# Sliding windows by DMA: staged batches in two half-block units instead of whole blocks, and one clear for all semaphores

## Chip, cores and metric

The kernel runs on 1 core of one Trainium2 chip. The metric is device time in microseconds (us), the median of several runs. Lower is better.

## What is computed

The input `x` holds 32 batches of 4096 rows of 256 float32 numbers. Every batch is cut into 127 windows of 64 rows that start 32 rows apart, so neighbouring windows overlap by half. The output is the list of windows:

```
def reference(x, window_size, stride):            # 64, 32
    batch, length, dim = x.shape                  # 32, 4096, 256
    n_windows = (length - window_size) // stride + 1        # 127
    result = np.zeros((batch, n_windows, window_size, dim), dtype=np.float32)
    for i in range(n_windows):
        start = i * stride
        result[:, i] = x[:, start:start + window_size].copy()
    return result
```

Nothing is calculated. A batch is 128 blocks of 32 rows (32 KB each, 4 MB in all). Window w is block w followed by block w + 1. A batch of output is 127 windows of 64 KB, that is 8.3 MB, and the whole output is 266 MB.

## The kernel before

The kernel consists of DMA transfers alone. It moves the batches in two ways.

**Copied batches.** Twenty of the 32 batches go from DRAM to DRAM. `copy` (L93) starts three DMAs for each of them on the SP queue, for 80, 32 and 15 windows. `COPY_PARTS` also says into how many pieces the 64 KB of a window are cut: 4, 2 and 4, which makes pieces of 16, 32 and 16 KB. Every byte of the output is then read from DRAM once, so most blocks are read twice.

**Staged batches.** Twelve batches (`STAGED`, the odd numbers 1 to 23) go through SBUF on the ACT queue. `load` (L75) brings the 128 blocks of a batch into one tile, one block of 32 KB in each partition. `store` (L83) waits until the tile has been loaded (L88) and writes it to DRAM twice: once into the first halves of the windows, once (half -1) into the second halves. Each DMA of a staged batch is 4 MB, and `start` (L61) cuts its 32 KB rows into pieces of 16 KB. There are five tiles (`BUFS`), used in turn; a load into a tile that was used before first waits (L79) until that tile's earlier stores have ended.

The ACT queue is written out in L139 to L148: load 0, then for each n load n + 1 followed by the two stores of n. One load is always issued ahead of the store that waits.

**The order between the two.** Written as 128 whole blocks, each store of a staged batch reaches a half window too far into the batch before it and the batch after it, and leaves a wrong block there. The neighbours, which are copied batches, put that right by being written later: on the SP queue, a copied batch next to a staged one waits (L137) until the staged batch's stores have ended. `_order` (L102) puts those copies where the wait should be short. Four batches (`EARLY`: 18, 20, 22, 24) are copied first instead, before their neighbours are stored; ACT waits for these once (L146). Their damaged blocks are repaired at the end of the SP queue by seven DMAs of 32 KB (`half`, L46, started in L152 to L158), each after the store that damages the block.

Every DMA adds 16 to a semaphore when it ends, in shares of one for every DMA engine that takes part. `loaded` and `stored` have one semaphore for each tile, and `copied` and `early` one each. At the end SP waits for all stores (L159) and all copies (L161), and clears the twelve semaphores one by one (L162, L163).

Names used below: the SP ring and the ACT ring are what the two queues (q1 and q10 of the profile) hold on each of the 16 DMA engines. A turn of a ring is one packet that it gets from an engine.

Of the kernel before, what the change touches and what calls it, by code (L numbers as in the profile page):

```python
# [1 line left out]

# [4 lines left out]


STAGED = tuple(range(1, 24, 2))
BUFS = 5  # L10

EARLY = (18, 20, 22, 24)

BLOCK_PARTS = 2

COPY_PARTS = ((80, 4), (32, 2), (15, 4))


class _Geometry:


    def __init__(self, x, out, W, S):
        self.B, self.L, self.D = x.shape
        self.x, self.out = x, out
        self.n_win = (self.L - W) // S + 1
        self.n_blk = self.L // S
        self.blk = S * self.D
        self.win = W * self.D
        assert W == 2 * S and self.n_blk == self.n_win + 1 == 128

    def src(self, b, block, dims):

        at = (b * self.n_blk + block) * self.blk
        return bass.AP(self.x.tensor, self.x.offset + at, dims)

    def dst(self, b, half, dims):

        at = b * self.n_win * self.win + half * self.blk
        return bass.AP(self.out.tensor, self.out.offset + at, dims)

    def rows(self, b, w0, n):

        s, d = [[self.blk, n], [1, self.win]], [[self.win, n], [1, self.win]]
        return self.dst(b, 2 * w0, d), self.src(b, w0, s)

    def half(self, b, half, block):  # L46

        dims = [[self.blk // 16, 16], [1, self.blk // 16]]
        return self.dst(b, half, dims), self.src(b, block, dims)


class _Kernel:
    def __init__(self, nc, g, tiles):
        self.nc, self.g, self.tiles = nc, g, tiles
        self.loaded = [nc.alloc_semaphore(f"loaded{i}") for i in range(len(tiles))]
        self.stored = [nc.alloc_semaphore(f"stored{i}") for i in range(len(tiles))]
        self.copied = nc.alloc_semaphore("copied")
        self.early = nc.alloc_semaphore("early")
        self.count = {}

    def start(self, engine, out, in_, sem, parts=1):  # L61
        engine.dma_start(out=out, in_=in_, max_dma_last_dim=65536 // parts).then_inc(sem, 16)
        self.count[id(sem)] = self.count.get(id(sem), 0) + 16

    def all_of(self, engine, sem):
        engine.wait_ge(sem, self.count[id(sem)])

    def slot(self, n):
        return divmod(n, len(self.tiles))

    def after_store(self, engine, n):
        turn, i = self.slot(n)
        engine.wait_ge(self.stored[i], 32 * (turn + 1))

    def load(self, n):  # L75

        g, (_, i) = self.g, self.slot(n)
        if n >= len(self.tiles):
            self.after_store(self.nc.scalar, n - len(self.tiles))  # L79
        src = g.src(STAGED[n], 0, [[g.blk, g.n_blk], [1, g.blk]])  # L80
        self.start(self.nc.scalar, self.tiles[i][:, :], src, self.loaded[i], 2 * BLOCK_PARTS)

    def store(self, n):  # L83

        g, (turn, i) = self.g, self.slot(n)
        self.nc.scalar.wait_ge(self.loaded[i], 16 * (turn + 1))  # L88
        for half in (0, -1):
            dst = g.dst(STAGED[n], half, [[g.win, g.n_blk], [1, g.blk]])  # L90
            self.start(self.nc.scalar, dst, self.tiles[i][:, :], self.stored[i], 2 * BLOCK_PARTS)

    def copy(self, b, sem):  # L93

        w = 0
        for rows, parts in COPY_PARTS:
            self.start(self.nc.sync, *self.g.rows(b, w, rows), sem, parts)
            w += rows
        assert w == self.g.n_win


def _order(B):  # L102


    near = {b for s in STAGED for b in (s - 1, s + 1)}
    order = list(EARLY) + [b for b in range(B) if b not in near and b not in STAGED]
    tied = sorted(near - set(EARLY))
    n = len(order) + len(tied)
    for b in tied:
        behind = max(STAGED.index(s) for s in (b - 1, b + 1) if s in STAGED)  # L110
        order.insert(-(-(2 * behind + 5) * n // (2 * len(STAGED))), b)
    return order


@with_exitstack
def kernel(
    ctx: ExitStack,
    tc: tile.TileContext,
    x: bass.AP,
    window_size: bass.AP,  # L120
    stride: bass.AP,
    out: bass.AP,
):
    nc = tc.nc
    W, S = int(window_size), int(stride)
    g = _Geometry(x, out, W, S)
    assert 0 not in STAGED and g.B - 1 not in STAGED
    pool = ctx.enter_context(tc.tile_pool(name="blocks", bufs=1))
    tiles = [pool.tile([g.n_blk, g.blk], x.dtype, name=f"xb{i}") for i in range(BUFS)]

    with tc.tile_critical():
        k = _Kernel(nc, g, tiles)
        for b in _order(g.B):
            if b not in EARLY:
                for s in (b - 1, b + 1):
                    if s in STAGED:
                        k.after_store(nc.sync, STAGED.index(s))  # L137
            k.copy(b, k.early if b in EARLY else k.copied)
        k.load(0)  # L139
        waited = False  # L140
        last = len(STAGED) - 1
        for n, s in enumerate(STAGED):
            if n < last:
                k.load(n + 1)
            if not waited and (s - 1 in EARLY or s + 1 in EARLY):
                k.all_of(nc.scalar, k.early)  # L146
                waited = True
            k.store(n)  # L148


        k.all_of(nc.sync, k.early)
        for n, s in enumerate(STAGED):  # L152
            if s - 1 in EARLY or s + 1 in EARLY:
                k.after_store(nc.sync, n)
            if s - 1 in EARLY:
                k.start(nc.sync, *g.half(s - 1, 2 * g.n_win - 1, g.n_blk - 1), k.copied)
            if s + 1 in EARLY:
                k.start(nc.sync, *g.half(s + 1, 0, 0), k.copied)  # L158
        for n in range(len(STAGED)):  # L159
            k.after_store(nc.sync, n)  # L160
        k.all_of(nc.sync, k.copied)  # L161
        for sem in [*k.loaded, *k.stored, k.copied, k.early]:  # L162
            nc.sync.sem_clear(sem)  # L163


# [1 line left out]
_INS = ['x', 'window_size', 'stride']  # L167
_OUTS = [((32, 127, 64, 256), 'float32')]

_NUMBERS = {'window_size': 64, 'stride': 32}  # L170


# [26 lines left out]
```

## Time and profile before

| | |
|---|---|
| runs before | 768.57, 766.97, 766.28 us; median 766.97 us |
| profiled execution | 768.4 us, of which the span of the instructions is 766.6 us |
| moved by DMA | 317.70 MB, mean 414 GB/s |
| SP queue (q1) | 10044 packets, 166.70 MB |
| ACT queue (q10) | 9792 packets, 151.00 MB |
| DRAM | 217.02 MB read, 267.35 MB written |
| busy time of the compute engines | 0.2 us (four fills on POOL) |

There is no compute engine to look at. The profile is read by its DMA part: the share of time that the 16 DMA engines are busy, the GB/s of chosen stretches, the packets of each queue, and the waits and issues on the two issuing engines, SP and ACT. The chain of work that ended last follows compute instructions and says nothing here.

### The profile page before, as it was taken

How to read it: one execution, taken by the hardware profiler on the slowest of the kernel's cores; microseconds unless marked ns; L12 is line 12 of the kernel's file. 1: busy time of each engine (PE TensorE's matmuls, PEld its weight loads, DVE VectorE, ACT ScalarE, POOL GpSimd, SP SyncE). 2: the span in 40 equal slices, each digit the busy share in tenths (PEclk: the TensorE clock that was granted, in tenths of full speed). 3: DMA queues.
4: the chain of work that ended last, by engine and by line, in shares of the span. 5: the costliest groups of instructions: out<-in, count | busy, mean ns of one | idle time of the engine just before them, and what ended most of it. 6: DMA issues, size and time to landing. Idle time of an engine off the chain costs nothing. (4 is left out here: it accounts for less than half of the span.)

```text
span 766.6 us, 180 instructions
## 1 busy us (share of the span) xinstructions
POOL 0.2 (0%) x4
## 2 busy tenths in 40 slices
POOL 0000000000000000000000000000000000000000
DMA  8999999999999999999999999999999999999996
GB/s 371 425 410 421 405 428 431 408 411 427 423 415 421 431 415 425 432 408 416 427 420 417 431 420 420 423 428 410 414 427 419 422 428 418 417 428 421 420 406 237
DMA packets 19837, 317.70 MB, mean 414 GB/s; under 512 B 1628, under 2 KB 1628, under 8 KB 1740
## 3 DMA queue, kind: packets, MB, share of 16 engines
q1 hardware_dynamic: 10044, 166.70, 51.9%
q10 hardware_dynamic: 9792, 151.00, 47.3%
q14 instruction: 1, 0.01, 0.0%
HBM read 217.02 MB, written 267.35 MB: 632 GB/s over the span
## 5 line engine op out<-in xcount | busy, mean ns | idle before, releaser
L180 POOL MEMSET const-bfloat16-1.0<- 128x1 bf16 x1 | 0.1, 102 | 0.0
L180 POOL MEMSET const-uint8-127<- 128x1 uint8 x1 | 0.1, 102 | 0.0
L180 POOL MEMSET const-float32-0.0<- 128x1 f32 x1 | 0.1, 99 | 0.2 <-issue 0.2
L180 POOL MEMSET const-float32-1.0<- 128x1 f32 x1 | 0.1, 99 | 0.0
## 6 DMA issues: line engine op xcount, KB each, us to landing
out_dram<-in_x_dram SPq DMA_DIRECT2D x20, 5120.0 KB, 114.8
out_dram<-xb ACTq DMA_DIRECT2D x24, 4096.0 KB, 84.6
xb<-in_x_dram ACTq DMA_DIRECT2D x12, 4096.0 KB, 123.2
out_dram<-in_x_dram SPq DMA_DIRECT2D x20, 2048.0 KB, 116.7
out_dram<-in_x_dram SPq DMA_DIRECT2D x20, 960.0 KB, 97.7
out_dram<-in_x_dram SPq DMA_DIRECT2D x7, 32.0 KB, 48.3
```

What stands on the lines that cost most here:

```text
L180: nc = _bacc.Bacc("TRN2", target_bir_lowering=False, num_devices=1)
```

## The change

A staged batch is no longer moved as whole blocks. Every block is cut in two halves of 16 KB (`BLOCK_PARTS` = 2 columns of the tile), and a unit is one half of all 128 blocks of a batch: 2 MB. The twelve staged batches become 24 units. A unit has a load, two stores, a `loaded` and a `stored` semaphore of its own, so there are ten slots in the same five tiles. The two halves of a batch follow each other. Two units are loaded ahead (`AHEAD` = 2) where one batch was before. The pieces of 16 KB stay as they are. Where SP waited for the stores of a batch, it now waits for both units (`after_batch`). The 22 semaphores, which have consecutive numbers, are cleared by one instruction.

```diff
+BLOCK_PARTS = 2
+AHEAD = 2
...
+        self.slots = len(tiles) * BLOCK_PARTS
+        self.size = g.blk // BLOCK_PARTS
+        self.loaded = [nc.alloc_semaphore(f"loaded{i}") for i in range(self.slots)]
+        self.stored = [nc.alloc_semaphore(f"stored{i}") for i in range(self.slots)]
...
-    def load(self, n):
-        g, (_, i) = self.g, self.slot(n)
-        if n >= len(self.tiles):
-            self.after_store(self.nc.scalar, n - len(self.tiles))
-        src = g.src(STAGED[n], 0, [[g.blk, g.n_blk], [1, g.blk]])
-        self.start(self.nc.scalar, self.tiles[i][:, :], src, self.loaded[i], 2 * BLOCK_PARTS)
+    def after_batch(self, engine, n):
+        for c in range(BLOCK_PARTS):
+            self.after_store(engine, n * BLOCK_PARTS + c)
+    def in_tile(self, unit):
+        t, c = divmod(unit % self.slots, BLOCK_PARTS)
+        return self.tiles[t][:, c * self.size : (c + 1) * self.size]
+    def in_dram(self, at, unit, step):
+        c = unit % BLOCK_PARTS
+        return bass.AP(at.tensor, at.offset + c * self.size, [[step, self.g.n_blk], [1, self.size]])
+    def load(self, unit):
+        g, i = self.g, unit % self.slots
+        if unit >= self.slots:
+            self.after_store(self.nc.scalar, unit - self.slots)
+        src = self.in_dram(g.src(STAGED[unit // BLOCK_PARTS], 0, [[1, 1]]), unit, g.blk)
+        self.start(self.nc.scalar, self.in_tile(unit), src, self.loaded[i])
+    def store(self, unit):
+        g, (turn, i) = self.g, divmod(unit, self.slots)
         self.nc.scalar.wait_ge(self.loaded[i], 16 * (turn + 1))
         for half in (0, -1):
-            dst = g.dst(STAGED[n], half, [[g.win, g.n_blk], [1, g.blk]])
-            self.start(self.nc.scalar, dst, self.tiles[i][:, :], self.stored[i], 2 * BLOCK_PARTS)
+            dst = self.in_dram(g.dst(STAGED[unit // BLOCK_PARTS], half, [[1, 1]]), unit, g.win)
+            self.start(self.nc.scalar, dst, self.in_tile(unit), self.stored[i])
...
-        k.load(0)
-        last = len(STAGED) - 1
-        for n, s in enumerate(STAGED):
-            if n < last:
-                k.load(n + 1)
+        for unit in range(AHEAD):
+            k.load(unit)
+        units = len(STAGED) * BLOCK_PARTS
+        for unit in range(units):
+            if unit + AHEAD < units:
+                k.load(unit + AHEAD)
+            s = STAGED[unit // BLOCK_PARTS]
...
-            k.store(n)
+            k.store(unit)
...
-        for sem in [*k.loaded, *k.stored, k.copied, k.early]:
-            nc.sync.sem_clear(sem)
+        used = sorted(sem.num for sem in [*k.loaded, *k.stored, k.copied, k.early])
+        nc.sync.sem_clear(range(used[0], used[-1] + 1))
```

## The prediction

> **What bounds the kernel now.** I read the page's DMA part first, since no compute engine works. It holds the busy share and the rate of 40 slices (19.2 us each), the packets and the two queues.
>
> ```profile
> DMA  8999999999999999999999999999999999999996
> GB/s 371 425 410 421 405 428 431 408 411 427 423 415 421 431 415 425 432 408 416 427 420 417 431 420 420 423 428 410 414 427 419 422 428 418 417 428 421 420 406 237
> q1 hardware_dynamic: 10044, 166.70, 51.9%
> q10 hardware_dynamic: 9792, 151.00, 47.3%
> ```
>
> The 16 DMA engines are busy 51.9 + 47.3 = 99.2% of 766.6 us, so 760 us, and only the first and last slices show slack. No wait on SP or ACT can be worth more than the remaining 6 us. What the change does to the busy time decides: the bytes, which stay, and the time of a packet. In the packet records of the trace the median packet of 16 KB takes 0.611 us in both queues, one of 32 KB 1.213 us. Summed over all packets, the time above these medians is 18.8 us per engine (sum divided by 16). So the rate in the slices varies between 405 and 432 GB/s, and I ask when it falls. Next I read the rate by stretches, in one cycle of ACT: load of staged batch 3 (ends 168), the two stores of batch 2 (190, 210), load of batch 4 (232). These times are the medians of the 16 completions of each DMA.
>
> ```profile
> 149.00:155.00 6.00, 0.00 (x0) 1.00 0.94 347
> 155.00:165.00 10.00, 0.00 (x0) 1.00 1.00 429
> 165.00:168.00 3.00, 0.00 (x0) 1.00 1.01 344
> 171.00:187.00 16.00, 0.00 (x0) 1.00 1.02 434
> 187.00:190.00 3.00, 0.00 (x0) 1.00 1.01 410
> 190.00:207.00 17.00, 0.00 (x0) 1.00 1.00 427
> 207.00:210.00 3.00, 0.00 (x0) 1.00 1.00 382
> 219.00:229.00 10.00, 0.00 (x0) 1.00 1.01 423
> 229.00:232.00 3.00, 0.00 (x0) 1.00 1.00 350
> 750.00:757.00 7.00, 0.00 (x0) 1.00 0.91 348
> 757.00:764.00 7.00, 0.00 (x0) 1.00 0.41 143
> ```
>
> The last two columns are DMA share and GB/s. Inside a load (429, 423) and inside the stores (434, 427) the rate is the same. It falls where ACT's ring turns: before the end of a load (344, 350), before the end of the second store (382), and after the start of a load (347). Where a store follows a store it hardly falls (410). I call this the cost of a turn of direction. The engines are as busy as before (share about 1.0), the packets of both rings take longer.
>
> At the end, SP's ring is alone from 750 on, slow (348), and then engines finish one after another.
>
> **The change, part by part.** ACT's order before: loads 0 and 1, stores 0, load 2, stores 1 and so on: 11 turns from load to store and 10 back. After: three loads, then two stores and one load in turn: 22 and 21. So 11 turns of each kind are added. The depth is the same: when ACT waits for a load to land, its ring holds two stores and a load behind it (12 MB), after the change four stores and two loads of half the size (12 MB). So no engine runs dry, and the wait on a tile (ten slots, 20 MB) is over long before.
>
> 1. Ends before a turn. I summed packet time above the medians, per engine, from 6 us before to about 2 us after the median completion: 0.47 us at a load's end (10 loads), 0.38 at the end of the second store (10), 0.09 at the end of the first store (11), which has no turn. A turn costs 0.38 + 0.29 over that, a pair 0.67; 11 pairs make +7.4 us, on all engines, thus on the path.
> 2. Starts of loads. From 1 to 12 us after the second store's end the same sum is 0.47 us (from 0.13 to 0.92), over some 0.1 at first stores. The new load lasts about 10 us instead of 20. Either each start costs the whole (11 x 0.36 = +4.0) or the loss belongs to the bytes and is only spread (0). I take the middle, +2.0.
> 3. Completions. 36 DMAs more, each with one 4-byte packet of 9 ns on each engine: +0.3 us.
> 4. One clear. The twelve start 59 ns apart, from 764.93 to 765.58, with nothing beside them: -0.65 us.
> 5. Who ends last. Chained end to start, the records show the engines alternate strictly between the rings, one packet each (an ACT packet followed the SP packet in 6,893 of some 7,600 cases), and a completion packet takes a whole turn. Before, ACT has 36 x (16 + 1) = 612 turns per engine, SP 20 x 28 + 60 = 620 and 14 small ones at the end. ACT starts 3.4 us, some 5 packets, ahead; so SP has 13 turns left alone, which is the stretch from 750 on. After, ACT has 72 x (8 + 1) = 648. SP ends first, and ACT has some 24 turns, 13 us, alone, all stores. ACT-alone stores are not in the trace: between 348 GB/s (nothing gained) and 428 (7 us x (1 - 348/428) = -1.3). I take -0.9, nearer the store rows.
> 6. The last two repairs of 32 KB. SP issues them when the last store has landed:
>
> ```profile
> SPq L62 <- DMA out_dram<-xb: 61.2, 2, 40.2
> SPq L66 <- DMA out_dram<-in_x_dram: 7.7, 1, 7.7
> ```
>
> The wait of 40.2 us ends at 755.3. The repairs then lie behind SP's own copies, whose last packet ends at 763.17, and they land at 764.86: 1.7 us later. With SP's ring empty that cover is gone: the second is issued 0.96 us after the wait, a packet starts 1.07 us after an issue (ACT's first: 0.91 to 1.98), and their packets took 0.08 to 1.3 us. That is 2.1 to 3.4 us after the last store, +0.4 to +1.7; I take +1.1.
>
> Cost nothing: the 36 more issues on ACT (0.44 us each, while its ring holds tens of us of work), and the longer chains of waits on SP at the end (one instruction in 65 ns, during the repairs' flight). SP's copies behind a staged batch wait longer, as ACT's data now falls behind by up to 36 turns, some 40 us by the end. Queued behind these waits are all later copies; the DMAs already in SP's ring hide it, as a copy's first DMA lands 114.8 us after its issue. Without that cover SP's engines' turns would go to ACT, and only the tail could lengthen.
>
> Sum: 7.4 + 2.0 + 0.3 - 0.65 - 0.9 + 1.1 = +9.2 us on 768.4, the profiled execution's time, so 777.6. That run lies 1.4 us above the median of the three; on the median's scale, 776.2.
>
> One rule speaks against the change more strongly. The Trainium skill, DMA: Bandwidth & Descriptors, section Anatomy of one DMA, fits a GpSimd-issued DMA by about 2.0 us fixed plus bytes over 436 GB/s. By that, 36 more DMAs would add 72 us if nothing covered them. The stretches across a store's end show a share of 1.00 or more, so no gap.
>
> The same page, section Queues, rings and completion order, says an engine drains a whole packet, typically 9 to 17 descriptors, from one ring before it switches. By that a half load (8 pieces) would pass in one go and point 5's count of turns would be wrong. The records of this trace alternate after every piece of 16 or 32 KB, and the measurement decides.
>
> **The rivals.**
> - Only the ends change (no rate change): the turns' cost belongs to the bytes loaded. Then +0.3 - 0.65 - 0.9 + 1.1 = -0.15: 766.8 on the median's scale. For it: the starts vary from 0.13 to 0.92. Against it: the inside of a load costs nothing, and the first store's end hardly anything.
> - Faster: engines no longer turn together. A load lasts 10 us per engine instead of 20. Where the spread of the 16 completions reaches that, only about a third of the engines load at a time, direction is mixed evenly, and the bursts of both ends go. Half of the present 13.2 us at turns (4.7 + 3.8 + 4.7 over 10 cycles) saved is -6.6: 760.2. It decides once the spread is about 10 us for most engines; load 5 landed between 291.4 and 300.7, but 14 of 16 within 2.8 us. That speaks against it.
> - Much slower by addresses: pieces of 16 KB are now 32 KB apart in the load and 64 KB apart in the stores, where pairs lay together. If all loads ran as the load's worst rows (347 instead of 412 GB/s over the 247 us of loads), +46 us, about 822. Nothing in the trace shows it, as pieces were separate packets already.
>
> **How the numbers follow.** A measurement of this kernel can tell about 0.3%, or 2.3 us, from no change. Chances: turns cost again, 0.68; only the ends, 0.15; mixing, 0.14; addresses, 0.03. The likeliest gives 776.2 us. Its own range: point 1 by 0.4 to 1.3 of its size (turns of short units may burst less, or both kinds longer), point 2 from 0 to 4.0, points 5 and 6 by their bounds, which is 769 to 782. The range for 8 in 10 reaches down over the second rival but not the third, and up a little: 764 to 783. Faster by over 0.3% (under 764.7): 0.14. Within: nearly all of the second rival and a little of the first, 0.16. Slower: 0.70.
>
> **What would show it.** Right: DMA share still over 99%, mean GB/s some 1% lower, slices more even and nearer 410 than 430, low stretches at the end of every half load; ACT's queue ends last; SP's last wait for stores ends a few us before the end and the wait for the copies (7.7 us) shrinks to 2 or 3; one clear. Wrong: slices at 425 and over (turns cost nothing, or less when mixed), idle DMA engines in the middle (the depth does not hold), or SP's ring alone at the end as before (point 5).

## The result and the profile after

The changed kernel takes 781.16 us (median of four runs, 779.7 to 781.9), against 766.97 us before. The ratio is 1.018, with a 95% interval of 1.0161 to 1.0198. The profiled execution took 781.9 us, its span is 780.1 us, 13.5 us more than before.

The page's DMA part of the changed kernel, with the busy share and the GB/s of 40 slices and the two queues:

```profile
DMA  9999999999999999999999999999999999999995
GB/s 376 409 421 410 403 419 402 419 413 412 416 394 425 411 417 418 407 423 412 413 422 402 431 394 426 402 414 418 422 418 413 410 420 407 414 418 400 413 403 221
q1 hardware_dynamic: 10044, 166.70, 51.7%
q10 hardware_dynamic: 10368, 151.00, 47.0%
```

SP's queue has the same packets as before, ACT's has 576 more (36 DMAs of 16 completions). The engines are busy 98.7% of 780.1 us, that is 770 us instead of 760. The rate rarely reaches the 425 to 432 that every second or third slice had before. The median packets are still 0.611 and 1.213 us; the sum of what packets take above these medians has gone from 18.8 to 29.3 us per engine.

The rate by stretches, in a cycle of the changed kernel (start and end, length, POOL, PE clock, DMA share, GB/s). By the medians of their completions, loads end at 131.5, 164.3 and 197.5, first stores of a unit at 141.8 and 174.7, second stores at 154.6 and 187.5. A row counts a packet where it starts, so a row whose share is off 1.00 is off in its rate too: with packets split at the edges, 183:188 gives 372 GB/s instead of 347, and the row 149:155 of the kernel before 371 instead of 347.

```profile
129.00:132.00 3.00, 0.00 (x0) 1.00 1.03 377
132.00:139.00 7.00, 0.00 (x0) 1.00 1.00 428
139.00:142.00 3.00, 0.00 (x0) 1.00 1.00 426
151.00:155.00 4.00, 0.00 (x0) 1.00 1.02 385
155.00:161.00 6.00, 0.00 (x0) 1.00 1.01 421
161.00:165.00 4.00, 0.00 (x0) 1.00 1.01 360
165.00:172.00 7.00, 0.00 (x0) 1.00 1.00 428
183.00:188.00 5.00, 0.00 (x0) 1.00 0.94 347
188.00:194.00 6.00, 0.00 (x0) 1.00 1.01 423
194.00:198.00 4.00, 0.00 (x0) 1.00 1.00 356
762.00:768.00 6.00, 0.00 (x0) 1.00 0.94 399
768.00:777.00 9.00, 0.00 (x0) 1.00 0.34 147
777.00:780.00 3.00, 0.00 (x0) 1.00 0.09 22
```

It is the picture of before, twice as often. The rate falls at the end of each load (377, 360, 356) and of each second store (385, and 347 or, split, 372), not where a store follows a store (426). A load here lasts 10 us. The beginning of a half load is hardly slow (421, 423).

The tail has changed sides. ACT's ring is alone from about 762, near full rate (399 GB/s with one engine of 16 already done). Then the other engines finish one after another from 766.8 to 776.3. The waits on SP (total, times, longest), and the clear (count, ns, first and last start):

```profile
SPq L77 <- DMA out_dram<-xb: 214.6, 10, 62.1
SPq L73 <- DMA out_dram<-in_x_dram: 0.8, 1, 0.8
```

```profile
L184 SPq EVENT_SEMAPHORE_RANGE_CLEAR  x1: 68/68/68, 779.1 to 779.1; - x1
```

SP now waits 214.6 us in all for stores, where it was about 80, yet the DMA engines stay busy through the middle of the run: the copies in its ring cover it. Its last wait for a store ends at 776.3, the last copy lands at 778.99, and one clear of 68 ns follows. The wait for the copies is down from 7.7 to 0.8 us.

### The profile page after: what moved, and what is told of

It is laid out like the page before. It is cut to its first block, busy times and chain, and to the rows that moved or that the text cites. A ratio compares the mean times of both kernels' runs of the same rounds, so it can differ in the third digit from the quotient of the medians.

```text
span 780.1 us, 223 instructions
## 1 busy us (share of the span) xinstructions
POOL 0.2 (0%) x4
## 3 DMA queue, kind: packets, MB, share of 16 engines
q1 hardware_dynamic: 10044, 166.70, 51.7%
```

## The experiments

The theory is that ACT's ring costs all engines time whenever it turns between loading and storing. The rivals are the addresses (pieces of 16 KB are no longer next to the other half of their block) and the number of DMAs. For each kernel I show the page's line of packets and mean rate; the median of the kernel before was 766.94 us beside the first four runs and 767.16 beside the other three.

**1. The same half units, loads and stores in pairs.** Number and addresses of the DMAs stay as in the changed kernel; the turns go back to 11.

```diff
-        for unit in range(units):
-            if unit + AHEAD < units:
-                k.load(unit + AHEAD)
...
-            k.store(unit)
+        for n, s in enumerate(STAGED):
+            for unit in range(2 * n, 2 * n + 2):
+                if unit + AHEAD < units:
+                    k.load(unit + AHEAD)
...
+            for unit in range(2 * n, 2 * n + 2):
+                k.store(unit)
```

> The changed kernel with its 24 half-block units, semaphores, sizes and single clear, but ACT's order in pairs: both halves of a batch are loaded, then both halves of the batch before are stored. 72 DMAs as in the changed kernel, 11 turns from load to store as before. Turn theory (each added pair of turns costs about 0.95 us of all engines): the packet time above the medians goes back from 29.2 to about 19 us per engine and the time to 767 to 771 us, the rest over 767 being the later end of ACT's ring. Address theory (pieces 32 or 64 KB apart are slow): stays at 780 to 782 us. DMA-count theory (each DMA's completion costs): stays at 780 to 782 us.

```profile
DMA packets 20414, 317.71 MB, mean 414 GB/s; under 512 B 2204, under 2 KB 2204, under 8 KB 2316
```

770.35 us, ratio 1.0046 (1.0029 to 1.0063); packet time above the medians 19.5 us. With the same packets as the changed kernel the rate is that of before. Addresses, number and all else that is not the order together leave 3.4 us of the 14.2; the other three quarters are the order.

**2. Units of whole blocks.** A unit is every second block of a batch instead of half of every block. The order and the turns stay; the lines not shown keep a unit at 64 rows and the pieces at 16 KB.

```diff
-        return self.tiles[t][:, c * self.size : (c + 1) * self.size]
+        return self.tiles[t][c::BLOCK_PARTS, :]
...
-        return bass.AP(at.tensor, at.offset + c * self.size, [[step, self.g.n_blk], [1, self.size]])
+        return bass.AP(at.tensor, at.offset + c * step, [[step * BLOCK_PARTS, self.size], [1, self.g.blk]])
```

> The changed kernel with units of another cut: every second whole block of 32 KB (64 rows in two pieces of 16 KB) in place of half of every block. Same 2 MB units, same order, 72 DMAs, same turns; the two pieces of a block lie together again. Turn theory: 779 to 783 us, as the changed kernel. Address theory: back to 767 to 771 us. DMA-count theory: 779 to 783 us.

```profile
DMA packets 20414, 317.71 MB, mean 407 GB/s; under 512 B 2204, under 2 KB 2204, under 8 KB 2316
```

781.65 us, ratio 1.0191 (1.0176 to 1.0206), 28.9 us above the medians: as the changed kernel. Where the pieces lie does not matter.

**3. Fewer turns than before.** The kernel before, with loads and stores of two batches at a time.

```diff
-            if n < last:
-                k.load(n + 1)
...
-            k.store(n)
+        for first in range(0, len(STAGED), 2):
+            for n in range(first + 2, min(first + 4, len(STAGED))):
+                k.load(n)
+            for n in range(first, first + 2):
...
+                k.store(n)
```

> The kernel before (whole blocks, 36 DMAs of 4 MB, twelve clears) with ACT's order in pairs of batches: two loads, then four stores. 5 turns from load to store instead of 11, 4 back instead of 10. Turn theory: 6 pairs less at 0.95 us each, -5.7 us: about 761 us. Address and DMA-count theories: 766 to 768 us, no change. If SP runs dry behind its waits for stores that now land later, more than 768 us with idle DMA engines in the middle.

```profile
DMA packets 19837, 317.70 MB, mean 417 GB/s; under 512 B 1628, under 2 KB 1628, under 8 KB 1740
```

761.49 us, ratio 0.9927 (0.9908 to 0.9946), 13.8 us above the medians: the 761 us of the turn theory, which also holds in this direction. SP waited longer for stores (188.7 and 86.5 us instead of 19.2 and 61.2) and the engines stayed busy.

**4. Quarter units.** As experiment 2, with `BLOCK_PARTS` and `AHEAD` at 4.

> Quarter units: every fourth whole block (32 rows of 32 KB, 1 MB per DMA), four units loaded ahead, 144 DMAs, 48 loads. Some 44 turns from load to store instead of 22 in the changed kernel and 11 before. Turn theory: 33 pairs more than before at 0.95 us = +31 us, +1 us for completions, some us for ACT's longer end: about 800 us, or less if bursts of turns only 5 us apart run together (then 785 to 795). Address theory: 767 to 772 us. DMA-count theory: 108 DMAs more, three times the added cost of the changed kernel, about 810 us.

```profile
DMA packets 21566, 317.72 MB, mean 404 GB/s; under 512 B 3356, under 2 KB 3356, under 8 KB 3468
```

787.39 us, ratio 1.026 (1.0239 to 1.0281), 31.6 us above the medians. The straight line (800 us) missed, and so did the count of DMAs (810 us). The weaker form written down beside it held: 22 turns more than in the changed kernel add only 2.3 us of packet time. A load of four packets per engine lasts about 5 us there, so the bursts that took 3 to 5 us at each turn have no room to be apart; this reason is argued from the lengths, not shown. SP's ring also ended near 740, so the last 40 us ran without copies.

**5. The staged batches alone.** The copied batches and repairs are taken out of the kernel before and of the changed kernel.

```diff
-        for b in _order(g.B):
-            ...
-            k.copy(b, k.early if b in EARLY else k.copied)
...
-        k.all_of(nc.sync, k.early)
-        ...
```

> The kernel before without its copied batches and their repairs: only the twelve staged batches, on ACT's ring alone (the twenty copied batches are left out of the output). Measures the turns by themselves, 11 and 10 of them. If a turn is slow in its own ring: the packet time above the medians stays at 10 us or more per engine. If a turn is slow only beside DRAM-to-DRAM copies: 3 us or less, and the time is about 576 packets x 0.607 us = 350 us plus some 8 us at the ends.

> The same cut made in the changed kernel: only the 24 staged half-block units, 22 and 21 turns. If a turn is slow in its own ring: some 10 us longer than the cut kernel before. If it is slow only beside copies: within 2 us of it.

Stretches of the cut kernel before: the last 2 or 3 us of two loads, which end at 52.8 and 82.2 and are followed by a turn (50:53, 80:82), and the longer stretches between, each with two stores and the turn back to a load. Then its rate by slices and that of the cut changed kernel:

```profile
24.00:50.00 26.00, 0.00 (x0) 1.00 1.01 432
50.00:53.00 3.00, 0.00 (x0) 1.00 0.99 415
80.00:82.00 2.00, 0.00 (x0) 1.00 0.97 377
82.00:110.00 28.00, 0.00 (x0) 1.00 1.01 432
```

```profile
GB/s 311 431 384 434 429 427 433 431 424 429 431 433 427 433 433 415 431 429 416 431 431 431 433 434 431 406 433 434 429 433 433 427 424 429 429 425 434 433 434 110
```

```profile
GB/s 312 379 434 417 433 422 427 434 424 420 434 413 436 418 426 429 434 431 429 424 427 431 431 429 424 418 431 433 429 424 422 431 431 429 420 426 431 433 230 34
```

363.84 and 370.06 us. With packets split at the edges the two load ends run at 420 and 391 GB/s, where beside copies load ends run at 345 to 362 by the same count. The packet time above the medians is 3.5 and 4.7 us: 1.3 us for eleven pairs of turns more, 0.12 us a pair, where beside copies it was (29.3 - 18.8) / 11 = 0.95 us. So of the packet time that a pair of turns costs, seven eighths come only beside the DRAM-to-DRAM copies. Whether other transfers in the second ring would do the same, no run shows. Yet the time grew by 6.2 us, against the 2 us that I had given this case. The last two slices (230, 34 against 434, 110) show where: the last store's 16 completions came from 354.9 to 360.3 us in the one kernel, and in the other thirteen from 355.5 to 356.4 and three later, at 360.6, 365.6 and 368.5. (The two stores of a unit count on one semaphore; the completions of the first, 4.9 us earlier on the same engine, are left out here.) These engines fell behind step by step: the last completion of a load came 1.4 us after the median at 107 us, and 12.8 us after it at 326. With the ring alone a few engines lose far more than the others, and the end waits for the last of them. This is one profile and two runs of each.

**6. Groups of three batches, and one clear.** Five loads, six stores, three loads, six stores and so on.

```diff
+        plan = [("L", n) for n in range(BUFS)] + [("S", n) for n in range(3)]
+        for first in (3, 6, 9):
+            plan += [("L", n) for n in range(first + 2, min(first + 5, len(STAGED)))]
+            plan += [("S", n) for n in range(first, first + 3)]
...
```

> The kernel before with ACT's order in groups of three batches (five loads, six stores, three loads, six stores and so on: 4 turns from load to store, 3 back) and one clear. Turn theory: 7 pairs less than before at 0.95 us = -6.6 us, and -0.65 us for the clear, so about 760 us. Rival: loads now wait for stores that have only just been issued and SP's copies wait longer, a ring runs dry and the time is 762 us or more with idle DMA engines in the middle.

```profile
DMA packets 19837, 317.70 MB, mean 420 GB/s; under 512 B 1628, under 2 KB 1628, under 8 KB 1740
```

Its longest row of waits on SP:

```profile
SPq L73 <- DMA out_dram<-xb: 228.6, 8, 39.6
```

758.86 us, ratio 0.9899 (0.9882 to 0.9915), 10.8 us above the medians: faster than both kernels. SP's waits are longer again (228.6 us) and nothing runs dry in the middle.

The packet time above the medians against the number of turns from load to store, all from profiles: 4 turns 10.8 us, 5 turns 13.8, 11 turns 18.8 and 19.5 (with 36 and 72 DMAs), 22 turns 29.3 and 28.9 (half blocks, whole blocks), 44 turns 31.6. Each figure is from one profile. The steps are not even (3.0 us from 4 to 5 turns), so 0.95 us for a pair is a mean over the step from 11 to 22.

## Why the prediction was right

Forecast +9.2 us, measured +14.2 us on the medians and +13.5 us between the profiled spans. The likeliest case happened, and the time lies inside its own range (769 to 782), near the upper end. Between the spans, the busy time grew by 10.5 us where 8.8 were forecast (points 1, 2, 3 and 5), and the rest by 3.0 where 0.45 were (points 4 and 6). That the range still held owes something to its width: two premises of the forecast, that no engine runs dry and that all engines are alike, did not hold. Of its signs, the DMA share fell to 98.7%, under the 99% named, and the mean rate by 1.7%, more than the 1% named.

- **Points 1 and 2, the turns.** Together +9.4 us were forecast; the packet time above the medians rose by 10.5 us, or 11.2 without SP's lone stretch at the end of the kernel before (point 5). The split was off. Summed over the same stretches, load ends went from 4.7 us (10 loads) to 13.9 (21), second stores' ends from 3.8 to 7.0, first stores' ends from 1.0 to 0.7: +12.1 us instead of +7.4. The starts gave less than nothing in return (-1.6 us by difference). In a load of 10 us the stretch before its end overlaps that after its start, so the two cannot be held apart as cleanly as in a load of 20 us. Experiments 1, 2 and 3 show that for most of it the order decides, not addresses or number.
- **Point 3, completions.** 576 more, 0.3 us per engine, as forecast. The Trainium skill, DMA: Bandwidth & Descriptors, section Anatomy of one DMA, would by its fixed 2.0 us, fitted to GpSimd-issued DMAs, have given 72 us uncovered (an estimate); experiment 1, with all 72 DMAs, is 3.4 us over the kernel before, so in a full ring the fixed part is covered.
- **Point 4, the clear.** From the end of the last wait to the end of the span: 766.63 - 764.86 = 1.77 us before, 780.12 - 778.99 = 1.13 after. -0.64 us, as forecast.
- **Point 5, who ends last.** Right: SP's regular copies ended near 762, ACT's ring at 776.3, 14 us later (13 forecast), and its stores alone lost nothing (median and mean packet 0.611 us), where SP's lone copies had lost 0.7 us per engine after 750; -0.9 was forecast. The 620 turns of SP hold for 15 engines only. SP's 10044 packets are 15 x 620 + 520 + 224 for the repairs, and the 940 completions of its copies are 20 x (16 + 16 + 15): the copy of 15 windows leaves one engine out, which so has 80 pieces, some 49 us of work (80 x 0.611), less than the others. From 720 on in the kernel before, 15 of 16 engines are busy (share 0.94 in the rows below), slack that the forecast's reading of the slices missed. That the idle one is the engine with fewer copies is inferred, as the records do not name engines. A more even cut of these copies is untried. The same page's section Queues, rings and completion order has an engine drain typically 9 to 17 descriptors before it switches; the strict alternation is seen again in the changed kernel's records (an ACT packet follows an SP piece of 16 KB in 7,509 of the 7,584 cases that can be told apart).
- **Point 6, the repairs.** They landed 2.7 us after the last store (2.1 to 3.4 forecast), 1.0 us more than before.
- **What was missing.** Span not covered by busy engines grew from 6.6 to 9.6 us. Repairs and clear explain +0.4 of these 3.0; I had nothing for the rest. About 0.8 us of it lies between 80 and 40 us before the end. Rows of the kernel before, then of the changed one:

```profile
710.00:720.00 10.00, 0.00 (x0) 1.00 1.02 436
720.00:730.00 10.00, 0.00 (x0) 1.00 0.94 401
730.00:740.00 10.00, 0.00 (x0) 1.00 0.94 405
```

```profile
710.00:720.00 10.00, 0.00 (x0) 1.00 0.94 375
720.00:730.00 10.00, 0.00 (x0) 1.00 0.94 388
730.00:740.00 10.00, 0.00 (x0) 1.00 1.01 429
```

In the changed kernel one engine runs dry from about 711 to 728 (15 of 16 is 0.94). It had its share of the last load at 691.1; the others got theirs from 717.7 to 727.4, and ACT issues the next stores only then, at 727.4. Another 1.6 us lies in the last 20 us. I took it for granted that a turn costs all engines alike. The last store's completions spread over 9.4 us (766.8 to 776.3), and over 5.0 us (758.2 to 763.3) with half the turns in experiment 1. In both I leave out the engine with fewer copies, which was done at 740.1 and 721.8. The uncovered span grows with the turns from load to store: 4.3 us with 4, 6.6 with 5, 6.6 and 6.5 with 11, 9.6 and 10.4 with 22, 13.1 with 44. That the turns make the ends uneven is argued from this, not shown.

Of the rivals, "only the ends change" gave 766.8 us. Experiment 1 shows what it would have needed, the order of before, though that run took 770.35 us. The 3.4 us that it lies over the kernel before are on the medians; its profiled run, the fastest of its four, has a span only 0.5 us longer than the profiled one of before, the slowest of its runs. What they are stays open. "Engines turn at different times" did not come; load 15's completions spread over 7.7 us, but the first 14 of 16 lay within 4.5 us, and bursts stayed. Experiment 4, where more turns cost little, may show some of it. The addresses are refuted by experiment 2.

Still open is why a turn costs this beside copies. The records show packets of both rings lengthening in the last 3 us or so of a load or second store. They do not show whether the loss is in the DRAM or in the DMA engines' own read and write sides.

## What to carry to other kernels

When the DMA engines are busy all the time, look at the rate in stretches of a few us and find the events at which it falls. Here those were changes between loading and storing, so long runs of one direction in a ring beat fine interleaving: 758.86 us with groups of three batches, 766.97 with one, 781.16 with halves. A cut into smaller DMAs by itself cost little here (at most 3.4 us, experiment 1); what matters is the order in which the smaller pieces are then put.

## What was not expected of the hardware

A pair of turns costs 0.95 us of packet time per engine beside DRAM-to-DRAM copies, and 0.12 us with the ring alone. The cost hardly grows when the turns come closer than their bursts are long (28.9 to 31.6 us from 22 to 44 turns). And with the ring alone it is uneven over the engines: thirteen of them ended within 0.9 us, and the last one 12.1 us after these.
